# A Hyena mixer with a mixture of experts on one core: where the norm of half of the tokens and the filter steps stand

## Chip, core and metric

The kernel runs on one core of a Trainium2 chip. The metric is the device time of one execution in microseconds (us). The engines are TensorE (PE, with its weight loads listed as PEld), VectorE (DVE), ScalarE (ACT), GpSimd (POOL) and SyncE (SP), which issues most of the DMAs. Each engine works through its own queue in order.

## What is computed

One layer on 2048 tokens of width 1024: positional embedding, adaLN norm, a Hyena mixer (projection to three streams, a convolution of three taps, two long convolutions by FFT with filters that a small network generates), then a mixture of experts. The part that matters here, cut from the reference:

```python
x = x + _grid_pos_embed(rows, D_MODEL)[None]
m_l = jnp.split((jax.nn.silu(c) @ mod_w[i] + mod_b[i])[:, None, :], 6, -1)
hl = _layer_norm(x, ADALN_EPS) * (1.0 + m_l[1]) + m_l[0]
u = _centred_conv3(hl @ w_in + b_in, conv_w, conv_b)          # 1024 -> 3072
v, x1, x2 = jnp.split(u, 3, -1)
# filters: a = sin(...) three times, h = (a @ f_w3) * window, two-sided, divided by its L1 norm, rfft
z = x2 * long_conv(x1 * long_conv(v, 0), 1)
x = _ln_affine(DEEPNORM_ALPHA * x + (1.0 + m_l[2]) * (z @ w_out + b_out), ln_g, ln_b)
```

## The kernel before

Matmuls that need float32 accuracy are made of three matmuls on a high and a low part (`mm3`); `split_const` makes the parts: a cast on ACT, then a subtraction on DVE. Work that is to overlap is written as Python generators which a driving loop advances step by step, so the order of each engine's queue is the order in which the loops call `next`.

The front of the kernel has four pieces:

- `filter_acts` and `early_mod`: the filter's small network and the first two rows of the modulation, with 32 loads of its weights.
- `side_steps`: the norm of the tokens. `norm` takes two tiles of 128 tokens by 1024 at a time (a group; eight groups): it loads x and the column part of the positional embedding (`pc`) by SP, adds two embeddings on POOL, takes statistics on DVE (`ln_stats`, `rstd` with a Sqrt on ACT) and scales the tile on DVE. `turn` transposes a group on PE into PSUM, ACT applies the modulation (`ht`), and the tokens of the first half (quarters 0 and 1) are split into `hh` and `hl` in SBUF, while those of the second half go to DRAM (`h2d`) by SP.
- `filter_steps`: 64 product steps (`gen`: eight matmuls `g`, DVE's product with the window `gw`, absolute values on ACT `ab`, sums `acc` on DVE and POOL, sum and difference `hb` on POOL and DVE) and 64 transform steps (`tran`: four matmuls `sp`, ACT's copy `ev`, stores to `fud`); after eight of each, `norms` adds the sums up. Each `yield` is a step; there are some 139 by the kernel's own count.
- `phase_in`: the input projection. Its first half (stage A in this text) goes over 24 blocks of 128 output columns (`project`: per block 2 x 8 x 3 matmuls into `ip`); a block has four slots, each after 12 matmuls, in which `slot` advances other work: the filter's rest and then `open_B`, the split of the next block's weights (`split_w`) and `post`, which convolves, transposes and stores the block before. Then the second half does the same with the tokens that `open_B` fetched from `h2d`.

Before, `build` runs all of `side_steps` and 104 filter steps beside it, ahead of `phase_in`; the 35 that are left, and then the ten steps of `open_B`, go over stage A's first 90 slots. From `phase_in` on the order is the written one (`manual_schedule`); ahead of it the compiler may reorder. PSUM: `f_ps` has two buffers each of `g` and `sp`, `sd_ps` two for transposes, `i_psA` two each of `ip` and `tp`.

Of the kernel before, what the change touches and what calls it, by code (L numbers as in the profile page):

```python
# [12 lines left out]
F32 = mybir.dt.float32  # L13
F32R = mybir.dt.float32r
# [3 lines left out]
AF = mybir.ActivationFunctionType  # L18
OP = mybir.AluOpType
# [9 lines left out]
ADALN_EPS = 1e-6  # L29
# [3 lines left out]
ES = 2  # L33
MB = 8
MV = 2
XB = 7
ENDA = 90
NF0 = 104
VB = 2
L1 = 2  # L40
L2 = 1
# [127 lines left out]
def split_const(nc, hi, raw, lo):  # L169
    nc.scalar.copy(hi, raw)  # L170
    nc.vector.tensor_tensor(lo, raw, f_(hi), OP.subtract)  # L171
# [309 lines left out]
        yield  # L481


def side_steps(tc, A, md, sg, ident, S, ones_f, ps, h2d, mod):


    nc = tc.nc
    hA = S.st.enter_context(tc.tile_pool(reuse_waits="tile", name="hA", bufs=1, side="right"))
    xv = A["x"][0].rearrange("(n1 n2) d -> n2 n1 d", n2=16)

    def norm(wk, grp):
        stat = wk.tile([128, 2, 2], F32, name="stat")
        xs = []
        for j in range(2):
            n2 = grp * 2 + j
# [10 lines left out]
        r = wk.tile([128, 2], F32, name="r")  # L506
        nb = wk.tile([128, 2], F32, name="nb")
        rstd(nc, wk, r, nb, stat, ADALN_EPS, 2)
        for j in range(2):
            nc.vector.tensor_scalar(xs[j], xs[j], r[:, j:j + 1], nb[:, j:j + 1], op0=OP.mult, op1=OP.add)  # L510
            yield
        ready.append((grp, xs))

    def turn(wk):
        grp, xs = ready.pop(0)
        q, h = divmod(grp, 2)
        if grp in (0, 2):
            S.hh.append(S.x16.tile([128, 8, 512], F32R, name="x") if q == 0 else hA.tile([128, 8, 512], F32R, name="hh"))
            S.hl.append(S.x16.tile([128, 8, 512], F32R, name="x") if q == 0 else hA.tile([128, 8, 512], F32R, name="hl"))
        cols = slice(h * 256, h * 256 + 256)  # L520
        for t in range(0, 8, 2):
            p = ps.tile([128, 2, 256], F32, name="sd")
            ht = wk.tile([128, 2, 256], F32, name="ht", bufs=2)
            for i in range(2):
                for j in range(2):
                    nc.tensor.transpose(out=p[:, i, j * 128:j * 128 + 128], in_=xs[j][:, (t + i) * 128:(t + i) * 128 + 128],
                                        identity=ident)
                nc.scalar.activation(ht[:, i], p[:, i], AF.Identity, scale=md[:, 1, t + i:t + i + 1],
                                     bias=md[:, 0, t + i:t + i + 1])
            if q < 2:  # L530
                split_const(nc, S.hh[q][:, t:t + 2, cols], ht, S.hl[q][:, t:t + 2, cols])
            else:
                nc.sync.dma_start(h2d[q - 2, :, t:t + 2, cols], ht)
            yield

    ready = []
    with tc.tile_pool(reuse_waits="tile", name="h_wk", bufs=2, side="right") as wk:
# [4 lines left out]
        yield  # L542
        for _ in mod:
            next(first, 0)
        for _ in first:
            pass
        for grp in range(8):
            nx = norm(wk, grp + 3) if grp < 5 else iter(())
            for n, _ in enumerate(turn(wk)):
                next(nx, 0)  # L550
                next(nx, 0)
                yield
            for _ in nx:
                yield
    S.wpA = S.st.enter_context(tc.tile_pool(reuse_waits="tile", name="i_wA", bufs=2, side="right"))
    S.w = split_w(nc, S.wpA, load_w(nc, A, S.wpA, S.cts[0]))


def load_w(nc, A, wp, ct):
# [12 lines left out]
def phase_in(tc, A, S, filt, fst, fps, invn, sg, rowd, wod, ident, ones_f, h2d, ued, ud, x1d, x2d):  # L572

# [3 lines left out]
    nc = tc.nc  # L577
    with ExitStack() as st:
# [11 lines left out]
        r = wkA.tile([128, 2, 128], F32, name="cv", bufs=3)  # L590
# [119 lines left out]
        more = filt_then_B()  # L710
        late = None
        for n, ct in enumerate(cts):
            nxt = []

            def slot(i):
                nonlocal raw
                at = 4 * n + i
# [12 lines left out]
        while active:  # L730
            step()
        for _ in more:
            pass
        stA.close()
        S.st.close()

# [965 lines left out]
def build(tc, A, out):  # L1702
    nc = tc.nc
    with ExitStack() as st:
# [25 lines left out]
        with tc.tile_pool(reuse_waits="tile", name="i_cst", bufs=1) as S.top, ExitStack() as S.st, ExitStack() as fst:  # L1730
            fps = S.st.enter_context(tc.tile_pool(reuse_waits="tile", name="f_ps", bufs=2, space=PSUM))
            fcst = fst.enter_context(tc.tile_pool(reuse_waits="tile", name="f_cst", bufs=1))
            afw = fcst.tile([128, T], F32R, name="afw")
            arv = fcst.tile([128, T], F32R, name="arv")
            with tc.tile_pool(reuse_waits="tile", name="sd_ps", bufs=2, space=PSUM) as sps:
                pools = [fst.enter_context(tc.tile_pool(reuse_waits="tile", name="f_in", bufs=2))]
                filt = filter_steps(tc, A, fcst, pools, fps, afw, arv, invn, fud)
                with tc.tile_pool(reuse_waits="tile", name="f_ld", bufs=1) as ld, \
                        tc.tile_pool(reuse_waits="tile", name="m_wk", bufs=2) as mk:
# [4 lines left out]
                    side = side_steps(tc, A, md, sg, ident, S, ones_f, sps, h2d, mod)  # L1744
                    for n, _ in enumerate(acts):
                        next(mod, 0)
                        if n == 15:
                            next(filt)
                        if n == ES:
                            next(side)  # L1750
                    next(side)
                pools.append(fst.enter_context(tc.tile_pool(reuse_waits="tile", name="f_wk", bufs=2)))
                S.left = 139
                for n, _ in enumerate(side):
                    for _ in range((n + 1) * NF0 // 28 - n * NF0 // 28):
                        next(filt)
                        S.left -= 1
            phase_in(tc, A, S, filt, fst, fps, invn, sg, rowd, wod, ident, ones_f, h2d, ued, ud, x1d, x2d)
# [32 lines left out]
```

## Time and profile before

| | us |
|---|---|
| median of three runs | 4122.95 |
| lowest, highest | 4119.94, 4126.99 |
| the profiled execution | 4124.47 |
| its span, first to last instruction | 4122.70 |

The profile is one execution. The table of stretches gives each engine's busy time in a stretch, the granted clock of PE (1.00 is 2.4 GHz), the mean busy share of the 16 DMA engines and the rate. Groups by line show how often an operation ran, its busy time and the mean of one in ns. Waits tell which engine stood idle and whose instruction released it. The timeline shows single instructions; the recorded end of a matmul is modelled, so the distance between starts tells more than its length.

### The profile page before, as it was taken

The numbers are of one execution on the slowest core, as the hardware profiler recorded it, in microseconds if no ns is written. First come the engines' busy times: TensorE is split into PE (matmuls) and PEld (weight loads), VectorE is DVE, ScalarE is ACT, GpSimd is POOL, SyncE is SP. The second block draws the span as 40 slices with busy tenths as digits, with TensorE's granted clock in tenths as the row PEclk, the third lists the DMA queues.
The fourth block names the chain that finished last, engine by engine and source line by source line (L and its number), as shares of the span: only waits on it lengthen the run. The fifth ranks groups of instructions, "written<-read, shape, count | busy, mean of one in ns | idle before, by whom it ended". The sixth has DMA issues, their size and how long they took to land.

```text
span 4122.7 us, 53152 instructions
## 1 busy us (share of the span) xinstructions
PE 3857.8 (94%) x19830; PEld 3163.6 (77%) x19830; DVE 2798.6 (68%) x4044; ACT 1959.5 (48%) x2897; POOL 1077.3 (26%) x1106
## 2 busy tenths in 40 slices
PE   6788999999999998947999999999999999999997
PEld 2445787777777887736888888888888888888896
DVE  6997544776977776785666666666666666656666
ACT  4555332333777652123555555555555555544443
POOL 4674221222577542130000000000000000015635
PEclk7999999999999999978999999999999999999999
DMA  7666454666989996444656665666566666656764
GB/s 192 184 207 180 125 160 165 198 206 199 289 252 276 266 288 194 158 164 135 205 195 206 198 200 194 204 204 194 195 204 204 194 198 202 204 191 210 240 228 163
DMA packets 645822, 831.75 MB, mean 202 GB/s; under 512 B 56883, under 2 KB 532803, under 8 KB 643260
## 3 DMA queue, kind: packets, MB, share of 16 engines
q1 hardware_dynamic: 576066, 678.56, 51.8%
q0 software_dynamic: 52512, 146.97, 12.2%
q10 hardware_dynamic: 16986, 2.83, 0.4%
q8 instruction: 156, 2.56, 0.3%
q14 instruction: 102, 0.84, 0.1%
HBM read 643.82 MB, written 150.75 MB: 193 GB/s over the span
## 4 chain that ended last, share of the span: by engine, by line
PE 73%; DVE 10%; issue 5%; POOL 5%; DMA 4%; ACT 2%; SPq 0%; ACTq 0%; POOLq 0%; DVEq 0%
PE ab L1491 19%; PE ab L1492 10%; PE acc L175 5%; PE acc L176 5%; PE acc L177 5%; PE ip L175 4%; PE ip L177 4%; PE ip L176 4%; PE op L175 1%; PE op L177 1%; PE op L176 1%; PE sp L336 1%; PE ab L177 1%; PE ab L176 1%; PE ab L175 1%
## 5 line engine op out<-in xcount | busy, mean ns | idle before, releaser
L1491 PE MATMUL ab<-xs,w3h 128*128 128x512 f32 x1664 | 600.4, 399 | 0.0
L1491 PE MATMUL ab<-xs,w1h 128*128 128x512 f32 x1664 | 598.0, 399 | 0.0
L1390 DVE TENSOR_TENSOR w2l<-w2r,w2h 128x2048 fp32r<-128x2048 f32 x126 | 297.5, 2361 | 267.2 <-ACT w2h L1389 267.2
L1492 PE MATMUL ab<-xs,w3l 128*128 128x256 f32 x1664 | 468.2, 281 | 0.0
L1492 PE MATMUL ab<-xs,w1l 128*128 128x256 f32 x1664 | 466.5, 280 | 0.0
L175 PE MATMUL acc<-w2h,hh 128*128 128x512 f32 x1024 | 404.2, 395 | 14.5 <-ACT hh L170 13.8
L176 PE MATMUL acc<-w2l,hh 128*128 128x512 f32 x1024 | 402.5, 393 | 0.0
L177 PE MATMUL acc<-w2h,hl 128*128 128x512 f32 x1024 | 399.8, 391 | 0.8 <-DVE hl L171 0.8
L1491 PEld LDWEIGHTS ab<-xs,w3h 128*128 128x128 f32 x1664 | 313.0, 188 | 76.4
L1491 PEld LDWEIGHTS ab<-xs,w1h 128*128 128x128 f32 x1664 | 313.0, 188 | 72.8
L1537 POOL DMA_INDIRECT accd<-y,idx x27 | 68.4, 2533 | 1103.1 <-DVE y L1531 1096.8
L1390 DVE TENSOR_TENSOR w1l<-w1r,w1h 128x2048 fp32r<-128x2048 f32 x126 | 300.9, 2388 | 62.7 <-ACT w1h L1389 62.5
L170 ACT CAST hh<-u 128x256 fp32r<-128x256 f32 x256 | 104.1, 407 | 479.1 <-DVE u L1514 479.1
L1492 PEld LDWEIGHTS ab<-xs,w1l 128*128 128x128 f32 x1664 | 314.2, 189 | 7.1
L1492 PEld LDWEIGHTS ab<-xs,w3l 128*128 128x128 f32 x1664 | 314.8, 189 | 0.0
L1495 DVE TENSOR_TENSOR u<-ab,u 128x256 f32<-128x256 f32 x416 | 174.6, 420 | 204.2 <-ACT u L1494 195.9
L1390 DVE TENSOR_TENSOR w3l<-w3r,w3h 128x2048 fp32r<-128x2048 f32 x126 | 292.9, 2324 | 19.0 <-ACT w3h L1389 19.0
L1389 ACT CAST w2h<-w2r 128x2048 fp32r<-128x2048 f32 x128 | 244.1, 1907 | 96.1 <-PE acc L177 86.5
L1389 ACT CAST w1h<-w1r 128x2048 fp32r<-128x2048 f32 x128 | 244.5, 1910 | 80.2 <-PE ab L1491 79.0
L1389 ACT CAST w3h<-w3r 128x2048 fp32r<-128x2048 f32 x128 | 244.6, 1911 | 68.3 <-PE ab L1491 66.2
L175 PEld LDWEIGHTS acc<-w2h,hh 128*128 128x128 f32 x1024 | 193.1, 189 | 61.3 <-ACT hh L170 15.7
L1494 ACT COPY u<-ab 128x256 f32<-128x256 f32 x416 | 153.0, 368 | 183.0 <-PE ab L1492 182.9
(403 smaller groups left out, 9260.6 us busy)
## 6 DMA issues: line engine op xcount, KB each, us to landing
w1r<-in_moe_w_dram SPq DMA_DIRECT2D x128, 1024.0 KB
w3r<-in_moe_w_dram SPq DMA_DIRECT2D x128, 1024.0 KB
w2r<-in_moe_w_dram SPq DMA_DIRECT2D x128, 1024.0 KB
fud<-ev SPq DMA_DIRECT2D x128, 256.0 KB
kr<-fud SPq DMA_DIRECT2D x64, 512.0 KB
bn<-ao POOLq DMA_DIRECT2D x248, 128.0 KB, 7.1
mw<-in_mod_w_dram SPq DMA_DIRECT2D x96, 256.0 KB
wraw<-in_hy_w_in_dram SPq DMA_DIRECT2D x48, 512.0 KB
```

Of the source, the lines that this page charges most:

```text
L170: nc.scalar.copy(hi, raw)
L175: nc.tensor.matmul(out, lhsT=ah, rhs=bh, start=start, stop=False)
L176: nc.tensor.matmul(out, lhsT=ah, rhs=bl, start=False, stop=False)
L177: nc.tensor.matmul(out, lhsT=al, rhs=bh, start=False, stop=stop)
L336: nc.tensor.matmul(p, lhsT=s1[:, th], rhs=hb[th], start=True, stop=(n0 > 0))
L1389: nc.scalar.copy(h, raw)
L1390: eng.tensor_tensor(l, raw, f_(h), OP.subtract)
L1491: nc.tensor.matmul(p, lhsT=ws[2 * j][:, k, fs], rhs=xs[:, k], start=(k == 0), stop=False)
L1492: nc.tensor.matmul(p[:, 0], lhsT=ws[2 * j + 1][:, k, fs], rhs=xs[:, k, 0], start=False, stop=(k == 7))
L1494: nc.scalar.copy(u, p[:, 1])
L1495: nc.vector.tensor_tensor(u, p[:, 0], u, OP.add)
L1537: nc.gpsimd.indirect_dma_start(out=accd, out_offset=at(idx, h), in_=y, in_offset=None, compute_op=OP.add)
```

## The change

- Of `side_steps`, only quarters 0 and 1 (the first half of the tokens) come ahead of `phase_in`, with no filter step beside them. A quarter (four tiles) is normed at a time rather than two tiles; there are eight buffers for x rather than seven.
- The scaling of the norm moves from DVE (`tensor_scalar`) to ACT (`activation`, Identity with scale and bias).
- Quarters 2 and 3 become 29 steps in slots 0 to 21 of stage A; their transposes use `i_psA`'s `tp` buffers.
- All filter steps after the first (131 calls) go over slots 22 to 87; `open_B`'s ten over slots 88 to 95.
- The working tiles of the filter's network and the modulation move to the other side of SBUF, the first block's weights are loaded ahead and split during the turn of quarter 1, and the pool `hA` is opened by `build`.

The core of the diff (arguments that are only passed on are left out):

```diff
-XB = 7
-ENDA = 90
-NF0 = 104
+XB = 8
+SA = 22
+SF = 88
...
-    def norm(wk, grp):
-        stat = wk.tile([128, 2, 2], F32, name="stat")
+    def norm(quarter):
+        stat = wk.tile([128, 4, 2], F32, name="stat")
...
-            nc.vector.tensor_scalar(xs[j], xs[j], r[:, j:j + 1], nb[:, j:j + 1], op0=OP.mult, op1=OP.add)
-            yield
+            nc.scalar.activation(xs[j], xs[j], AF.Identity, scale=r[:, j:j + 1], bias=nb[:, j:j + 1])
+            yield 1
...
-        first = chain(norm(wk, 0), norm(wk, 1), norm(wk, 2))
-        next(first)
-        yield
-        for _ in mod:
-            next(first, 0)
-        for _ in first:
-            pass
-        for grp in range(8):
-            nx = norm(wk, grp + 3) if grp < 5 else iter(())
-            for n, _ in enumerate(turn(wk)):
-                next(nx, 0)
-                next(nx, 0)
-                yield
-            for _ in nx:
-                yield
+        for half in range(2):
+            first = norm(2 * half)
+            next(first)
+            yield 1
+            for _ in mod:
+                next(first, 0)
+            for _ in first:
+                if half:
+                    yield 1
+            nx = norm(2 * half + 1)
+            for n, _ in enumerate(turn(2 * half)):
+                next(nx, 0)
+                if n % 2:
+                    next(nx, 0)
+                yield 1
+            for _ in nx:
+                yield 1
+            for _ in turn(2 * half + 1):
+                yield 1
+            if half == 0:
+                yield None
...
+        psum[0] = lambda: psA.tile([128, 4, 128], F32, name="tp").rearrange("p (i j) c -> p i (j c)", i=2)
...
-        def filt_then_B():
-            yield from filt
+        def steps_of_A():
+
+            yield 0, SA, 29, side
+            open_filt()
+            yield SA, SF, 131, filt
             fst.close()
-            yield from open_B()
+            yield SF, 96, 10, open_B()
...
-                for _ in range((at + 1) * (S.left + 10) // ENDA - at * (S.left + 10) // ENDA):
+                a, b, count, more = part
+                for _ in range((at + 1 - a) * count // (b - a) - (at - a) * count // (b - a)):
                     next(more, 0)
+                if at == b - 1:
+                    for _ in more:
+                        pass
+                    part = next(plan, None)
...
+                S.wpA = S.st.enter_context(tc.tile_pool(reuse_waits="tile", name="i_wA", bufs=2, side="right"))
+                rawA = load_w(nc, A, S.wpA, S.cts[0])
+                for n, _ in enumerate(iter(lambda: next(side), None)):
+                    if n == 8:
+                        S.w = split_w(nc, S.wpA, rawA)
...
-                S.left = 139
-                for n, _ in enumerate(side):
-                    for _ in range((n + 1) * NF0 // 28 - n * NF0 // 28):
-                        next(filt)
-                        S.left -= 1
```

## Rows read from the trace of the kernel before

**Rows 1.** The page: span, and PE's busy tenths in 40 equal slices.

```profile
span 4122.7 us, 53152 instructions
...
PE   6788999999999998947999999999999999999997
```

**Rows 2.** Stretches: length, busy us (instructions) by engine, clock, DMA share, GB/s.

```profile
64.00:374.00 310.00, 236.83 (x932) 131.65 (x931) 290.19 (x388) 173.86 (x326) 213.72 (x137) 0.91 0.65 196
523.70:684.90 161.20, 161.20 (x749) 133.38 (x748) 77.12 (x115) 53.87 (x82) 34.29 (x50) 1.00 0.44 139
374.30:684.90 310.60, 309.46 (x1406) 248.25 (x1407) 149.84 (x213) 107.48 (x170) 76.98 (x97) 0.99 0.43 132
```

**Rows 3.** Stretches of the projection's own tile ip: PE, PEld and ACT busy.

```profile
523.70:684.90 161.20, 151.14 (x643) 118.90 (x642) 17.94 (x26) 1.00 0.44 139
```

**Rows 4.** PE's waits from 64 to 374 us: total us, times, longest.

```profile
PE g L295 <- DVE gw L298: 26.1, 25, 3.2
...
PE sp L336 <- POOL hb L312: 11.2, 15, 1.1
```

**Rows 5.** Timeline of PE at several moments: start us, us, instruction.

```profile
236.68 0.28 PE L296 MATMUL g<-wl,afw 128*128 128x256 f32 x1
236.80 0.28 PE L295 MATMUL g<-wh,afw 128*128 128x256 f32 x1
...
378.21 0.63 PE L175 MATMUL ip<-x,wh 128*128 128x512 f32 x1
378.63 0.63 PE L176 MATMUL ip<-x,wh 128*128 128x512 f32 x1
...
385.19 1.02 PE L336 MATMUL sp<-hb,s 128*128 128x512 f32 x2
...
498.66 1.89 PE L319 MATMUL g<-acc,onec 128*1 128x256 f32 x8
...
502.30 0.60 PE L614 MATMUL tp<-ident,cv 128*128 128x128 f32 x4
...
519.67 0.59 PE L336 MATMUL sp<-hb,s 128*128 128x512 f32 x1
```

**Rows 6.** Groups by line, 64 to 374 us: busy us, mean ns, idle before.

```profile
L312 DVE TENSOR_TENSOR hb<-gw,gw 128x512 f32<-128x512 f32 x58 | 78.7, 1357 | 0.2
L298 DVE TENSOR_TENSOR gw<-g,win 128x512 f32<-128x512 f32 x118 | 76.6, 673 | 6.6 <-PE g L296 6.4
...
L276 DVE TENSOR_TENSOR acc<-acc,ab 128x512 f32<-128x512 f32 x50 | 50.8, 1017 | 1.3 <-ACT ab L308 1.3
...
L528 ACT ACTIVATE ht<-sd,md 128x256 f32<-128x256 f32 x64 | 35.5, 565 | 31.5 <-PE sd L526 18.0 <-DVE hl L171 7.9 <-DVE x L171 4.9
...
L510 DVE TENSOR_SCALAR x<-x,r,nb 128x1024 f32<-128x1024 f32 x16 | 20.6, 1325 | 0.0
...
L170 ACT CAST x<-ht 128x512 fp32r<-128x512 f32 x8 | 4.8, 616 | 0.2
```

**Rows 7.** Line L312, whole span: ns shortest/median/longest, first and last start.

```profile
L312 DVE TENSOR_TENSOR hb<-gw,gw x64: 676/1750/1780, 65.5 to 473.7; 128x512 f32<-128x512 f32 x64
L312 POOL TENSOR_TENSOR hb<-gw,gw x64: 1260/1654/2262, 65.5 to 473.3; 128x512 f32<-128x512 f32 x64
```

**Rows 8.** Timeline near the first norm: POOL's adds, DVE's first scaling.

```profile
60.67 1.26 POOL L500 TENSOR_TENSOR x<-x,pr 128x512 f32<-128x512 f32 x1 [2.31 <-DMA x<-in_x_dram]
...
68.50 1.26 POOL L500 TENSOR_TENSOR x<-x,pr 128x512 f32<-128x512 f32 x1
...
70.94 1.26 POOL L500 TENSOR_TENSOR x<-x,pr 128x512 f32<-128x512 f32 x1
...
77.63 2.90 DVE L510 TENSOR_SCALAR x<-x,r,nb 128x1024 f32<-128x1024 f32 x2
```

**Rows 9.** Line L1569, the same scaling at the kernel's end: ns shortest/median/longest.

```profile
L1569 ACT ACTIVATE xs<-xs,nb,r x20: 1225/1236/1246, 3710.0 to 4069.5; 128x1024 f32<-128x1024 f32 x20
```

**Rows 10.** Tile hr, the second half's tokens fetched in stage A.

```profile
L695 SPq DMA_DIRECT2D hr<-h2d x8: 320/532/1001, 527.6 to 588.2; - x8
```

More of the change, by code (lines that the diff above doesn't have):

```diff
@@ L481, in early_mod, with side_steps @@
         yield
-def side_steps(tc, A, md, sg, ident, S, ones_f, ps, h2d, mod):
+def side_steps(tc, A, md, ident, S, psum, h2d, mod):
     nc = tc.nc
-    hA = S.st.enter_context(tc.tile_pool(reuse_waits="tile", name="hA", bufs=1, side="right"))
     xv = A["x"][0].rearrange("(n1 n2) d -> n2 n1 d", n2=16)
-    def norm(wk, grp):
-        stat = wk.tile([128, 2, 2], F32, name="stat")
+    def norm(quarter):
+        stat = wk.tile([128, 4, 2], F32, name="stat")
         xs = []
-        for j in range(2):
-            n2 = grp * 2 + j
+        for j in range(4):
+            n2 = quarter * 4 + j
             x = wk.tile([128, 1024], F32, name="x", bufs=XB)
@@ L512, in norm @@
[L512 to L533, printed above, removed]
-            yield
@@ new lines, in norm, with turn @@
+            yield 1
+        r = wk.tile([128, 4], F32, name="r")
+        nb = wk.tile([128, 4], F32, name="nb")
+        rstd(nc, wk, r, nb, stat, ADALN_EPS, 4)
+        for j in range(4):
+            nc.scalar.activation(xs[j], xs[j], AF.Identity, scale=r[:, j:j + 1], bias=nb[:, j:j + 1])
+            yield 1
+        ready.append(xs)
+    def turn(q):
+        xs = ready.pop(0)
+        if q < 2:
+            S.hh.append(S.x16.tile([128, 8, 512], F32R, name="x") if q == 0 else S.hA.tile([128, 8, 512], F32R, name="hh"))
+            S.hl.append(S.x16.tile([128, 8, 512], F32R, name="x") if q == 0 else S.hA.tile([128, 8, 512], F32R, name="hl"))
+        for h in range(2):
+            cols = slice(h * 256, h * 256 + 256)
+            for t in range(0, 8, 2):
+                p = psum[0]()
+                ht = wk.tile([128, 2, 256], F32, name="ht", bufs=2)
+                for i in range(2):
+                    for j in range(2):
+                        nc.tensor.transpose(out=p[:, i, j * 128:j * 128 + 128],
+                                            in_=xs[2 * h + j][:, (t + i) * 128:(t + i) * 128 + 128], identity=ident)
+                    nc.scalar.activation(ht[:, i], p[:, i], AF.Identity, scale=md[:, 1, t + i:t + i + 1],
+                                         bias=md[:, 0, t + i:t + i + 1])
+                if q < 2:
+                    split_const(nc, S.hh[q][:, t:t + 2, cols], ht, S.hl[q][:, t:t + 2, cols])
+                else:
+                    nc.sync.dma_start(h2d[q - 2, :, t:t + 2, cols], ht)
+                yield 1
@@ L536, in side_steps @@
     ready = []
-    with tc.tile_pool(reuse_waits="tile", name="h_wk", bufs=2, side="right") as wk:
+    with tc.tile_pool(reuse_waits="tile", name="h_wk", bufs=2) as wk:
         pr = wk.tile([128, 512], F32, name="pr", bufs=1)
         nc.sync.dma_start(pr, A["c_posr"])
-        first = chain(norm(wk, 0), norm(wk, 1), norm(wk, 2))
-        next(first)
-        yield
-        for _ in mod:
-            next(first, 0)
-        for _ in first:
-            pass
-        for grp in range(8):
-            nx = norm(wk, grp + 3) if grp < 5 else iter(())
-            for n, _ in enumerate(turn(wk)):
+        for half in range(2):
[9 more added lines that the diff above has]
+            for n, _ in enumerate(turn(2 * half)):
@@ L550, in side_steps @@
                 next(nx, 0)
-                next(nx, 0)
-                yield
+                if n % 2:
+                    next(nx, 0)
+                yield 1
             for _ in nx:
-                yield
-    S.wpA = S.st.enter_context(tc.tile_pool(reuse_waits="tile", name="i_wA", bufs=2, side="right"))
-    S.w = split_w(nc, S.wpA, load_w(nc, A, S.wpA, S.cts[0]))
+                yield 1
+            for _ in turn(2 * half + 1):
+                yield 1
+            if half == 0:
+                yield None
@@ L703, in open_B @@
                     yield
-        def filt_then_B():
-            yield from filt
+        def steps_of_A():
+            yield 0, SA, 29, side
+            open_filt()
+            yield SA, SF, 131, filt
             fst.close()
-            yield from open_B()
-        more = filt_then_B()
+            yield SF, 96, 10, open_B()
+        plan = steps_of_A()
+        part = next(plan)
         late = None
@@ L731, in phase_in @@
             step()
-        for _ in more:
-            pass
         stA.close()
@@ L1734, in build @@
             arv = fcst.tile([128, T], F32R, name="arv")
+            S.hA = S.st.enter_context(tc.tile_pool(reuse_waits="tile", name="hA", bufs=1, side="right"))
             with tc.tile_pool(reuse_waits="tile", name="sd_ps", bufs=2, space=PSUM) as sps:
@@ L1737, in build @@
                 filt = filter_steps(tc, A, fcst, pools, fps, afw, arv, invn, fud)
-                with tc.tile_pool(reuse_waits="tile", name="f_ld", bufs=1) as ld, \
-                        tc.tile_pool(reuse_waits="tile", name="m_wk", bufs=2) as mk:
+                psum = [lambda: sps.tile([128, 2, 256], F32, name="sd")]
+                with tc.tile_pool(reuse_waits="tile", name="f_ld", bufs=1, side="right") as ld, \
+                        tc.tile_pool(reuse_waits="tile", name="m_wk", bufs=2, side="right") as mk:
                     mod = early_mod(nc, A, md, sg, ident, ones_f, mk, sps)
```

12 lines of the change are left out of this document (5 added, 7 removed).

## The prediction

> **What bounds the kernel now.** The page comes first: TensorE (PE) is busy in nine tenths of the span except in a few slices, and the widest gap lies in slices 1 to 4, the first 400 us [rows 1]. Nothing in the diff touches code that runs after the input projection's first half, so I cut that front into stages by the table of stretches. Two stages matter. The *side stage*, 64 to 374 us, runs the norm of all 2048 tokens, its transposes and most of the filter: there VectorE (DVE) is busy 290.19 of 310 us and PE's records cover 236.83 [rows 2]. *Stage A*, 374.3 to 684.9 us, is the projection of the first half of the tokens with what is left of the filter: PE is busy 309.46 of 310.60 us, DVE only 149.84 [rows 2]. So DVE bounds the one, PE the other, and each leaves the other engine's time unused.
>
> A busy PE is not a full PE, so I price PE's work by the distance between starts. A projection matmul costs, its share of transposes and first DFT included, 161.20 us over 643 of them, 0.2507 us, in the stretch without filter [rows 2, 3]; 1152 cost 289 us. A filter matmul of 256 columns starts 0.12 us after the one before, two of 512 columns end 1.02 us after the start of the first, where one takes 0.59, so 0.43 apart; eight of the norm sums take 1.89, 0.22 each [rows 5]. The whole filter is 512 x 0.118 + 256 x 0.43 + 64 x 0.216 and some 14 us of one-row matmuls: 198 us. A transpose is about 0.11 [rows 5]. In the side stage lie 58 of 64 product steps (hb x58 [rows 6]), with 468 + 224 + 56 of those matmuls and 12 us, and 128 transposes: 189 us of work in 310. **PE has 121 us of slack there**, and its longest waits are for gw, which DVE makes, and for hb of POOL [rows 4]. That slack is what can be won.
>
> **The change, part by part.** *Lead-in.* Before the first projection matmul only quarters 0 and 1 of the tokens (8 tiles of 1024 columns) are still normalised and turned; no filter step stands among them. GpSimd (POOL) starts on the second tile at 60.67 and needs 1.26 for each of two adds, 2.44 a tile at its best [rows 8]: the eighth is done near 78, the fourth near 68. Its statistics and the reciprocal root of the quarter follow; before, the first scaling began at 77.63, for want of the slow small DVE operations beside POOL's adds [rows 8]. I take 75. From there ScalarE (ACT) is last. The scaling that it takes over from DVE costs 1.24 by the same operation at the kernel's end [rows 9], against 1.33 on DVE [rows 6]; 8 tiles are 9.9 us. A turn step is two scalings of 0.57 and a cast of 0.62 [rows 6]; 16 steps are 28 us. With the cast of the first weights, 39 us: 114, and 3 us for gaps between steps, so the projection starts at **117** rather than 374.3. Bounds: 110 if the root is ready at 71 and nothing gaps, 125 if each step waits 0.4 us more for PE and DVE. The loads of these tiles (6 MB) are no later than before, in the same order on SyncE's queue.
>
> *Stage A.* It now carries the projection (289), the whole filter (198) and 64 transposes (7): **494 us of PE work**, 183 more than the 311 now. If PE never waited, it would end at 117 + 494 = 611 against 684.9. What it waits for, in the order of the slots (a slot is 12 projection matmuls, 3.0 us):
>
> - The clock. Before, after the thinly filled side stage, projection matmuls stood 0.42 apart instead of 0.23 for a few us [rows 5]; eight of them cost 1.6 us. After a thinner lead-in the same: 2.
> - Slots 0 to 21 hold the second half's 29 side steps: 16 x loads and positional loads on SyncE behind the weight loads, POOL's adds ahead of POOL's DMA issues for the projection, statistics on DVE ahead of the weight split and the convolution, and 16 stores of turned tiles on SyncE. DVE stands in order behind POOL behind a DMA. Slots last 3.2 us and DVE's own share is near 2.2 (149.84 over 96 slots is 1.6, and 8 tiles' statistics at some 1.6 us over 22 slots are 0.6), so a late tile delays it by some us, once or twice. The bounds are 0 and 12; I take 5.
> - Slots 22 to 87 hold all filter steps, one product step and one transform step a slot. PE needs 66 x 3.0 + 198 = 396 us. DVE: a product step is two gw at 0.67, one hb and seven eighths of an acc at 0.68 undisturbed [rows 6, 7], with small things 2.8 us, 181 for 64; the projection's own DVE work is stage A's 149.84 less its filter and hB splits (34), two thirds of it 80. On top comes what POOL takes from DVE: hb is 0.68 alone and 1.75 beside a POOL operation [rows 7], 1.36 and 1.02 on the mean for hb and acc [rows 6], so 58 x 0.68 + 50 x 0.34 = 56 us lost over 108 POOL operations, 0.52 each. There are 120 in the new stretch: 62 at that rate, 128 if each blocks DVE in full (1.07). Small operations and the scaling lost time as well, so I take 85. DVE is 346 of 396, 87%, at most 389. In the side stage DVE reached 94%, so PE should keep the lead; for slots in which weight split, convolution and product step meet I add 14 us (bounds 3 and 40). ACT (174 + 107 busy in the two stages [rows 2], plus 20 for scaling) has half of the time free. DMA traffic is 310 x 196 + 311 x 132 GB/s, 102 MB, now in 575 us: 177 GB/s, under the 196 of the side stage.
> - Slots 88 to 95 hold the 10 steps that fetch and split the second half's turned tokens. Before, the fetches were issued from 527.6 to 588.2 [rows 10]; now in 24 us, with two buffers, by 8 casts on ACT's queue ahead of the projection's evacuations. Bounds 0 and 16; I take 7.
>
> That is 28 us: stage A ends at 117 + 494 + 28 = 639, **46 us earlier**. After it nothing changes. The scaling's removal from DVE (16 x 1.33 = 21 us) is worth nothing by itself in stage A and is in the lead-in already.
>
> A page speaks against the overlap: the Trainium skill, "SBUF — State Buffer", section "SBUF: two separate sides", says that the port pair shared by VectorE and GpSimd is an exclusive lock, so that the second to come blocks until the first is through. The rows agree with the lock (0.68 against 1.75). By the rule, a POOL add could hold DVE for the whole of its 1.26 us, and the two-input convolution operations would be exposed as well; 120 such blocks would be 151 us, DVE 412, and at 94% a stretch of 438 in place of 410: 4106 instead of 4078. The DVE-bound rival below is this mechanism, priced from rows alone.
>
> **The rivals.** *Clean overlap.* PE never waits beyond the lower bounds: start at 113, 10 us of waits, end 617, gain 68: 4057. For it: in stage A before, PE lost 2 us in all although filter steps ran beside it (309.46 of 310.60 [rows 2]). Against it: there were a quarter as many per slot.
>
> *DVE becomes the bound of the filter's slots.* POOL blocks it in full, DVE has 389, and at the side stage's 94% the slots last 416; PE's own waits (20) do not fall together with DVE's. With the start at 122 and 14 elsewhere: 122 + 494 + 40 + 14 = 670, gain 15: 4110.
>
> *PE stalls in every slot (slower).* The mechanism is order: in each slot PE's queue holds transform and product matmuls that need hb, gw's buffers and ev of the slots before, and while it waits, the projection matmuls behind cannot pass. In the side stage this cost 121 us for 58 product steps, 2.1 each. If each of 64 slots lost 2.1 us, 134 us in place of 14, the end would be 759: 4199. It decides from 54 us more than I count, 0.8 us a slot more. Against it: a product step's results are wanted a slot (6 us) later here, where in the side stage they were wanted at once, with DVE behind.
>
> *The change does not shorten the front*, because the loads of x and not the norm set the start: then 6 MB at the side stage's 196 GB/s, 31 us from 56, end at 87, ahead of ACT's 114. So this decides nothing.
>
> **How the numbers follow.** The profiled execution took 4124.47, 1.8 us outside its span, 1.5 over the median of the three runs (4122.95). 4124.5 - 46 = 4078.5; I say 4078. Chances: forecast 0.52, clean overlap 0.20, DVE-bound 0.20, stalls in every slot 0.08. Range: from 4055 (just past the clean case) to 4112 (past the DVE-bound one); what is left out is the slower case, and little on either side. Faster or slower counts from 0.2%, 8 us, about what a measurement of this kernel can tell from no change. Forecast and clean overlap are faster; of the DVE-bound case three quarters are. Faster 0.87, within 0.2% 0.05, slower 0.08.
>
> **What would show it.** Right: projection matmuls (ip) from 110 to 125 on; PE busy throughout from there to about 640; the filter's first hb near 190 and its last fud store near 610; DVE at 85 to 92% in between; PE's waits for gw, hb and ev under 15 us in total. A start later than 125 would put the error in the lead-in; waits of PE for DVE in most slots would speak for the DVE bound; a hole of 10 us or more near 640, before the second half's first matmul, for the fetches crowded into slots 88 to 95. I would be wrong altogether if stage A took more than 568 us.

## The result and the profile after

The changed kernel takes 4152.94 us (4150.83 to 4157.21) against 4123.88 of the kernel before in the same comparison: ratio 1.0072, interval 1.0055 to 1.0090. It is **29 us slower**, where the prediction said 46 faster. The profiled execution of after took 4150.83, with a span of 4148.5.

The page of after, its span, PE's busy tenths and PE's granted clock in 40 slices of 104 us, answers to [rows 1]:

```profile
span 4148.5 us, 53057 instructions
...
PE   5689998999999998966999999999999999999997
...
PEclk7899999999999998987999999999999999999999
```

The gap of slices 1 to 4 has become shorter and deeper (5, 6, 8 instead of 6, 7, 8, 8), and a dip at the seventh slice (8, from 622 to 726 us) is new; the notch at the eighteenth is in both. So the front was shortened, and yet the end came later: the loss lies in that slice and where the digits read 9, too fine for this view. The table of stretches, cut at the prediction's stages, shows it (columns as in [rows 2]):

```profile
64.00:115.40 51.40, 19.60 (x65) 9.35 (x65) 31.44 (x58) 35.34 (x59) 20.82 (x16) 0.50 0.43 143
115.40:240.00 124.60, 91.21 (x401) 71.58 (x402) 40.27 (x76) 47.88 (x79) 29.62 (x31) 0.89 0.38 120
240.00:680.00 440.00, 413.08 (x1809) 287.30 (x1808) 330.79 (x402) 207.00 (x358) 225.44 (x181) 0.97 0.55 166
680.00:703.00 23.00, 18.59 (x75) 15.01 (x74) 10.98 (x14) 7.99 (x10) 2.60 (x4) 0.85 0.58 184
703.00:760.00 57.00, 45.04 (x194) 35.33 (x193) 33.00 (x56) 16.51 (x24) 7.33 (x11) 0.91 0.77 265
```

The projection starts at 115.4 (predicted 117). Then PE stands still for 33 us in slots 0 to 21, for 26 in the filter's slots, for 4.4 in slots 88 to 95 (a transpose that waits for DVE's `cv`, at 691.6) and for 10 at the start of the second half. DVE, which could have been the bound of the filter's slots, is busy 330.79 of 440 us there, 75%: neither engine is full. The milestones, as predicted and in the trace of after, in us:

| | predicted | after | difference |
|---|---|---|---|
| first projection matmul | 117 | 115.4 | -2 |
| slots 0 to 21 | 80 | 119.8 (to 235.2) | +40 |
| slots 22 to 87 | 410 | 443.5 (to 678.7) | +33 |
| slots 88 to 95, up to the second half's first matmul | 31 | 29.6 (to 708.3) | -1 |
| from there to the second half's second block | 13.1, as before | 21.5 (to 729.8) | +8 |

The waits of PE in after, by stretch (115.4 to 240, 240 to 680, 680 to 760 us; total us, times, longest), stand beside those of [rows 4]:

```profile
PE tp L525 <- ACT ht L527: 26.3, 16, 9.6
PE sp L175 <- ACT vh L626: 6.6, 1, 6.6
...
PE g L319 <- DVE acc L276: 26.3, 8, 6.0
PE g L295 <- DVE gw L298: 0.3, 1, 0.3
...
PE ip L175 <- ACT ub L672: 10.5, 1, 10.5
```

These are three kinds of place, and gw, which led [rows 4] with 26.1 us, is down to 0.3. At each of them a short dependent step stands in PE's in-order queue, with projection matmuls ready behind it; whether the engines lack time all the same is what the experiments ask.

**Slots 0 to 21.** Each step of the turn issues two transposes, ACT's scaling of them, two more transposes into the other half of the same PSUM tile, and ACT's scaling again. The timeline of after at one step, with nothing else late (start us, us, engine, line, operation; in brackets the idle time before it and what ended it):

```profile
163.88 0.54 PE L525 MATMUL tp<-ident,x 128*128 128x128 f32 x2
...
164.46 0.56 ACT L527 ACTIVATE ht<-tp,md 128x256 f32<-128x256 f32 x1 [4.01 <-PE tp L525]
...
165.08 0.44 PE L525 MATMUL tp<-ident,x 128*128 128x128 f32 x2 [0.66 <-ACT ht L527]
```

The second pair can't start until ACT has read the first: about 1 us from start to start, 16 times, once for each step of the second half's turn. The Trainium skill, "PSUM — Partial Sum Buffer", section "PSUM bank collisions raise a hardware error", says why such a wait can't just be dropped: one engine may not write a PSUM bank while another reads it in the same partitions, whichever columns they touch (the tile is 4 x 128 float32 a partition, 2 KiB, by that page one bank). The trace agrees: ACT's read ends at 165.02, the next transpose starts at 165.08.

When ACT is late as well, the step costs far more. The longest such wait is 9.6 us, from 185.8 on. The other long wait of the stretch has the same chain, here from its beginning:

```profile
135.24 0.38 SPq L564 DMA_DIRECT2D wraw<-in_hy_w_in_dram  x1
...
135.71 0.53 SPq L496 DMA_DIRECT2D x<-in_x_dram  x1
...
140.37 1.26 POOL L499 TENSOR_TENSOR x<-x,pr 128x512 f32<-128x512 f32 x1 [7.25 <-DMA x<-in_x_dram]
...
141.67 0.69 DVE L378 BATCH_NORM_STATS2 bst<-x 128x6 f32<-128x512 f32 x1 [3.06 <-POOL x L499]
...
145.55 1.24 ACT L509 ACTIVATE x<-x,nb,r 128x1024 f32<-128x1024 f32 x1 [1.28 <-DVE nb L397]
146.70 0.56 ACT L626 CAST vh<-tp 128x512 fp32r<-128x512 f32 x1
...
147.31 0.80 PE L175 MATMUL sp<-vh,s1h 128*128 128x512 f32 x1 [6.60 <-ACT vh L626]
```

x is issued behind a weight load, POOL adds when it lands, DVE takes statistics, ACT waits in order for their root and then does the moved scaling, and only then the cast that PE wants. The cast has nothing to do with the norm; it is merely behind it on ACT.

**Slots 22 to 87.** All eight waits for acc are the norm sums, one for each of the filter's blocks. The timeline of after around one of them:

```profile
387.56 1.21 DVE L171 TENSOR_TENSOR wl<-wraw,wh 128x1024 fp32r<-128x1024 f32 x1
...
390.06 0.75 DVE L642 SCALAR_TENSOR_TENSOR cv<-ub,prm,cv 128x512 f32<-128x512 f32 x1
390.72 1.28 DVE L298 TENSOR_TENSOR gw<-g,win 128x512 f32<-128x512 f32 x2
...
391.71 1.28 POOL L276 TENSOR_TENSOR acc<-acc,ab 128x512 f32<-128x512 f32 x1
391.92 2.83 DVE L276 TENSOR_TENSOR acc<-acc,ab 128x512 f32<-128x512 f32 x1
...
392.93 1.26 POOL L312 TENSOR_TENSOR hb<-gw,gw 128x512 f32<-128x512 f32 x1
...
394.90 3.57 PE L319 MATMUL g<-acc,onec 128*1 128x256 f32 x8 [6.05 <-DVE acc L276]
```

DVE has the split of the projection's weights and the convolution ahead of the block's last gw and sum, and PE's next instruction is the sum over that sum. A filter block is eight product and eight transform steps, at two steps a slot eight slots, which is two projection blocks of four slots: so **every** block's last sum meets the same two jobs. The eight waits differ all the same, from 0.6 to 6.0 us.

**The boundary.** The fetches of the second half's tokens and the weights behind them on SP's queue, in after:

```profile
680.59 29.88 SPq L699 DMA_DIRECT2D hr<-h2d  x8
...
710.52 1.05 SPq L753 DMA_DIRECT2D x<-in_c_s_dram  x1
...
712.15 0.67 SPq L564 DMA_DIRECT2D wraw<-in_hy_w_in_dram  x1
...
728.16 1.04 ACT L170 CAST wh<-wraw 128x1024 fp32r<-128x1024 f32 x1 [11.94 <-DMA wraw<-in_hy_w_in_dram]
```

The same weights and cast in before:

```profile
686.24 0.43 SPq L561 DMA_DIRECT2D wraw<-in_hy_w_in_dram  x1
...
702.28 1.04 ACT L170 CAST wh<-wraw 128x1024 fp32r<-128x1024 f32 x1 [10.56 <-DMA wraw<-in_hy_w_in_dram]
```

Before, the last fetch was issued at 588.2 [rows 10] and the weights for the second half's second block 4.6 us ahead of that half's first matmul; now the fetches go on to 710.5 and the weights follow at 712.15, 3.8 us behind that matmul (708.3). ACT waits for them with an evacuation of ip behind, and PE waits 10.5 for that evacuation instead of 2.1. The late issue is one half of this. The other is that these weights need 16 us from issue to cast in both traces, where the page of after gives a median of 4.1 from issue to landing for this load over the whole kernel: right ahead of them on SP's queue go two tables of 2 MB each (`in_c_s`, `in_c_a`), in before too. That they wait for those tables is likely and was not tested.

### The profile page after: what moved, and what is told of

It reads as the page before. It is cut to its first block, busy times and chain, and to the rows that moved or that the text cites. A ratio compares the mean times of both kernels' runs of the same rounds, so it can differ in the third digit from the quotient of the medians.

```text
span 4148.5 us, 53057 instructions
## 1 busy us (share of the span) xinstructions
PE 3856.6 (93%) x19830; PEld 3169.5 (76%) x19830; DVE 2780.3 (67%) x4000; ACT 1980.2 (48%) x2909; POOL 1066.3 (26%) x1106
## 3 DMA queue, kind: packets, MB, share of 16 engines
q10 hardware_dynamic: 16986, 2.83, 0.5%
## 4 chain that ended last, share of the span: by engine, by line
PE 70%; DVE 11%; issue 6%; POOL 5%; DMA 5%; ACT 3%; SPq 0%; POOLq 0%; ACTq 0%; DVEq 0%
PE ab L1503 19%; PE ab L1504 9%; PE acc L175 5%; PE acc L176 5%; PE acc L177 5%; PE ip L175 3%; PE ip L177 3%; PE ip L176 3%; PE sp L336 2%; PE op L175 1%; PE op L177 1%; PE op L176 1%; PE ab L177 1%; PE ab L176 1%; PE ab L175 1%
## 5 line engine op out<-in xcount | busy, mean ns | idle before, releaser
L175 PE MATMUL ip<-hh,wh 128*128 128x512 f32 x576 | 235.8, 409 | 10.5 <-ACT ub L672 10.5
```

Source lines behind the costliest of these rows:

```text
L175: nc.tensor.matmul(out, lhsT=ah, rhs=bh, start=start, stop=False)
```

## The experiments

Two theories. **Order**: the work fits, and PE stands at the few places above, because a short dependent step is next in its queue. Then a change of order alone, with the same work, brings the time back. **Load**: there is too much for DVE, POOL and ACT beside PE in stage A, and order moves the waits about but not the sum. A difference below is taken against the 4152.94 of after, and a ratio with its interval against the kernel before of the same round. The intervals reach 4 to 7 us to either side, so a difference of a few us is not told from none.

### Both pairs of transposes ahead of ACT's scalings

```diff
                         nc.tensor.transpose(out=p[:, i, j * 128:j * 128 + 128],
...
+                for i in range(2):
                     nc.scalar.activation(ht[:, i], p[:, i], AF.Identity, scale=md[:, 1, t + i:t + i + 1],
```

> The kernel after, with one edit: in a turn step all four transposes are issued before ACT's two scalings, not two and two. Theory Order (PE stands in its queue behind short dependent steps): of 26.3 us of PE's waits for ht in slots 0 to 21, about 17 are the second pair of a step waiting for ACT's read of the first pair in the same PSUM tile; they go, with some 5 us of half clock behind them, and the lead-in loses up to 5: 20 to 27 us faster than the kernel after, 4126 to 4133. Theory Load (the engines beside PE cannot keep up with what was moved, and PE waits wherever it stands): the same wait turns up at the next transposes or casts, gain under 5, at least 4148.

4140.36 us, ratio 1.0034 (1.0022 to 1.0045): **13 us** back, between the two. The sixteen waits are gone from PE's list, and the filter's first matmul comes at 223.4 instead of 238.1. Some of it moved: the late x now shows in waits for the low part vl (6.1 us at 168.9) and for cv (6.8 at 190.7), which had cost next to nothing in these slots, beside the 6.8 for vh, so Order's size was about twice what came.

### x of the later quarters loaded ahead

```diff
+    def load(n2):
+        x = wk.tile([128, 1024], F32, name="x", bufs=XB)
+        nc.sync.dma_start(x, xv[n2])
+        return x
...
+    def norm(quarter, ahead=False):
...
+        if ahead:
+            got = [load(quarter * 4 + j) for j in range(4)]
...
+            yield 1
...
+            for n, _ in enumerate(turn(2 * half + 1)):
+                if half == 0 and n == 3:
+                    ahead = norm(2, True)
+                    next(ahead)
```

Quarter 2's x goes out in the turn of quarter 1, quarter 3's in slot 0; the positional loads run two tiles ahead.

> The kernel after, with one edit: the loads of x of quarters 2 and 3 are issued ahead (quarter 2's during the turn of quarter 1, quarter 3's in slot 0), the positional columns two tiles ahead, so that they do not stand behind the projection's weight loads on SyncE. Theory Order: the two long waits in slots 0 to 21 (7.0 us at 140, 9.9 at 186) are a late tile that holds POOL, DVE, ACT and then PE; they go, with 5 us of half clock: 15 to 22 faster, 4131 to 4138. Theory Load: DVE and ACT are late by their own work; gain under 5, at least 4148.

4140.67, ratio 1.0035 (1.0023 to 1.0046): **12 us** back, somewhat under the expected 15 to 22. PE's wait for vh falls from 6.6 to 1.2, the longest within a turn step from 9.6 to 3.1; fifteen short ones remain, and the norm sums are as they were (27.3 us). The filter starts at 228.7.

### The filter's steps two slots earlier

```diff
-SA = 22
-SF = 88
+SA = 20
+SF = 86
```

Not one instruction is added or taken away; only the slot in which each filter step meets the projection's.

> The kernel after, with all filter steps two slots earlier (slots 20 to 85 instead of 22 to 87); nothing else. The last sums of a filter block are then issued in slot 3 of a projection block, where DVE has neither the weight split nor the convolution of four rows, rather than in slot 1 behind both. Theory Order (the norm matmuls wait because DVE's sum stands behind that block's other work): PE's 26 us of waits at the eight norms fall under 10, with 8 us of half clock behind them, and the boundary gets 6 us more: 25 to 35 faster, 4118 to 4128. Theory Load (DVE and POOL are slow throughout the filter's slots): waits as long, only at other slots, and the crowded side steps (29 in 20 slots) cost some: 4148 to 4158. The variant with later norm matmuls was slower since their PSUM tile is one of gw's two, so PE then stood behind gw of the same slot; this one leaves that order alone.

4120.26, ratio 0.9992 (0.9982 to 1.0001): **33 us** back, the number that Order said, and level with the kernel before. Its waits of PE from 64 to 760 us, two lines:

```profile
PE tp L525 <- ACT ht L527: 18.7, 16, 5.0
...
PE g L319 <- DVE acc L276: 10.5, 5, 2.6
```

The 66 slots of the filter in after, then in this run (columns as in [rows 2]):

```profile
235.20:678.70 443.50, 416.58 (x1827) 290.32 (x1827) 334.47 (x408) 208.05 (x359) 226.30 (x182) 0.97 0.56 167
```

```profile
223.20:656.30 433.10, 412.92 (x1823) 289.90 (x1821) 337.31 (x407) 208.59 (x360) 227.50 (x182) 0.99 0.56 170
```

The waits for the norm sums cost 10.5 instead of 26.3, with as many slots and as much work as in after. But only a part of the gain lies there. In the profiled execution (4126.28, 24.5 less than that of after) the filter's slots give 10.4 of it, since new waits for gw, invn and ev (8.5 together) take some back. The rest lies in the side steps, whose waits for ht fell too (18.7 instead of 26.3), in the last slots and at the boundary (7.2 instead of 10.5). So the size came out as Order said, partly at other places than it named. That order alone, with the same instructions, brings 33 us back speaks against Load most plainly.

### The three together

```diff
-SA = 22
-SF = 88
+SA = 20
+SF = 86
...
+                for i in range(2):
...
+                    ahead = norm(2, True)
```

> The kernel after with three edits together: transposes of a turn step issued in one go, x of quarters 2 and 3 loaded ahead, filter steps two slots earlier. Theory Order: the three waits are separate places in PE's queue, so the gains add: 13 and 12 as measured and 25 to 35 for the phase, 48 to 60 faster than the kernel after: 4093 to 4105, faster than the kernel before. Theory Load: one lack shows up at three places, the gains do not add: at least 4125.

4096.4, ratio 0.9931 (0.9914 to 0.9947): 56.5 us less than after, where 13, 12 and 33 add to 58. **The three gains add**, as far as the intervals tell. The stretches of slots 0 to 19 (up to the filter's first matmul) and of the filter:

```profile
111.60:199.40 87.80, 77.30 (x364) 62.24 (x365) 37.47 (x67) 44.33 (x77) 27.61 (x29) 0.96 0.46 145
199.40:626.00 426.60, 409.48 (x1812) 287.94 (x1812) 335.91 (x409) 207.48 (x357) 226.91 (x180) 0.99 0.57 173
```

and two of PE's waits from 64 to 760 us:

```profile
PE g L319 <- DVE acc L276: 8.8, 5, 2.6
PE ip L175 <- ACT ub L697: 8.4, 1, 8.4
```

DVE does about the same work in less time (335.91 of 426.60 us, 79% against 75%), and PE waits less. Load would have it the other way. The mean granted clock in these two stretches is 0.96 and 0.99 where after has 0.89 and 0.97.

### The norm sums issued a step later

```diff
-        yield
         m = n - GA
-        if 0 <= m + 1 < 64 and steps[m + 1][1] == 7:
-            sums_of = norms(steps[m + 1][0])
+        if m >= 0 and steps[m][1] == 7:
+            sums_of = norms(steps[m][0])
             next(sums_of)
+        yield
         if m >= 0:
             tran(m)
```

> The kernel after, with one edit: the eight matmuls that add up a block's absolute sums (norms) are issued one step later, behind the product step and not ahead of the transform step, so DVE and POOL have some 3 us more (and the next product step's time) for the last sums. Theory Order: PE's 26.3 us of waits for acc go nearly all, and about 10 us of half clock that follows them: 28 to 36 faster, 4117 to 4125. Theory Load (DVE is the bound of the filter's slots): PE waits as long at other places, for gw or hb; gain under 8, at least 4145.

4163.55, ratio 1.0086 (1.0069 to 1.0103): **11 us slower** than after by the medians (6 by the ratios, whose intervals overlap), and no gain in any case; the expectation missed. PE's waits from 64 to 760 us say why:

```profile
PE g L319 <- DVE gw L298: 31.4, 7, 6.0
...
PE g L295 <- DVE gw L298: 4.9, 7, 1.6
```

The sums now come behind the next step's eight product matmuls, and their PSUM tile is one of the two named g. They no longer wait for acc but for DVE to empty a g that has just been filled. A wait moved along the same queue met the next dependence; that the sums wait for the block's last acc is only the first of two.

### All four quarters ahead, the filter over slots 0 to 87

```diff
-            if half == 0:
-                yield None
+    yield None
...
-            yield 0, SA, 29, side
             open_filt()
-            yield SA, SF, 131, filt
+            yield 0, SF, 131, filt
```

> The kernel after with all four quarters normalised and turned ahead of the projection (no side steps in stage A) and the filter's 131 steps over slots 0 to 87, 1.5 a slot. It separates the two things that the change moved into stage A. The lead-in grows by 8 scalings and 32 half steps on ACT, 28 us, plus gaps: start near 147. Theory Order: the 51 us of excess in slots 0 to 21 go, the norm waits fall since a block's sums have more time at 1.5 steps a slot: 25 to 45 faster than the kernel after, 4108 to 4128. If the filter's slots are what is slow at any density (Load): their excess of 44 us stays, gain 10 to 20, 4133 to 4143.

4143.54, ratio 1.0046 (1.0029 to 1.0062): 9 us better than after, and Order's number missed; it lies at the edge of Load's. The trace tells which term failed: the projection starts at 164.3, 49 us later than in after for two more quarters. PE's waits from 64 to 760 us:

```profile
PE sd L525 <- ACT ht L527: 43.6, 35, 5.5
...
PE g L319 <- DVE acc L276: 19.4, 7, 4.3
```

In a lead-in with nothing beside it, the turn's PE and ACT steps take turns and their waits are path. And the norm sums still wait 19.4 us, though the filter runs at 1.5 steps a slot instead of 2: thinning the load by a quarter doesn't remove them, which two slots of shift brought to 10.5. So the run speaks for neither theory by its time, and for Order by its waits.

### The scaling's engine

Three kernels. After, with the scaling back on DVE:

```diff
-            nc.scalar.activation(xs[j], xs[j], AF.Identity, scale=r[:, j:j + 1], bias=nb[:, j:j + 1])
+            nc.vector.tensor_scalar(xs[j], xs[j], r[:, j:j + 1], nb[:, j:j + 1], op0=OP.mult, op1=OP.add)
```

> The kernel after, with the norm's scaling put back on DVE. If ACT's queue is what holds the lead-in (ACT-bound by my sum) and the transposes of slots 0 to 21 (ht behind four scalings of 1.24 us), the start comes up to 8 us earlier and the wait of 9.6 us at 186 shrinks by 3: 6 to 12 us faster than the kernel after, 4141 to 4147. If DVE beside POOL's adds is as slow at it (1.33 us each before), nothing: within 4 of 4153.

4140.86, ratio 1.0040 (1.0026 to 1.0054): **12 us** less than after. The projection starts 1.4 us sooner (114.0), and the filter 9.6 sooner (228.5): the gain is for the most part in slots 0 to 21, where ACT has ht and the projection's evacuations behind the scaling and DVE has little to do.

The kernel before, with that one edit the other way round (DVE to ACT, two tiles at a time):

```diff
-            nc.vector.tensor_scalar(xs[j], xs[j], r[:, j:j + 1], nb[:, j:j + 1], op0=OP.mult, op1=OP.add)
+            nc.scalar.activation(xs[j], xs[j], AF.Identity, scale=r[:, j:j + 1], bias=nb[:, j:j + 1])
```

> The kernel before, with one part of the change alone: the norm's scaling on ACT rather than DVE. Theory DVE-bound side stage: 16 scalings of 1.33 us leave DVE's 290 of 310 us; 14 to 21 faster, 4103 to 4110. Rival (the chain through PE, POOL and ACT is as long as DVE's work, or ACT's queue order delays ht and ev): within 5 of the kernel before.

4118.3, ratio 0.9981 (0.9972 to 0.9991): **7.6 us faster** than before. The projection starts at 368.5 instead of 374.3. That lies between the two expectations: of some 21 us of work taken from DVE a third came back, so DVE was not the only bound of the side stage, or ACT's added work took the rest. The same edit is a gain there, and a loss where DVE has time.

The three reorderings with the scaling on DVE:

```diff
-            nc.scalar.activation(xs[j], xs[j], AF.Identity, scale=r[:, j:j + 1], bias=nb[:, j:j + 1])
+            nc.vector.tensor_scalar(xs[j], xs[j], r[:, j:j + 1], nb[:, j:j + 1], op0=OP.mult, op1=OP.add)
```

> The three edits together (transposes in one go, x ahead, filter two slots earlier: 4096) and the norm's scaling on DVE. On the kernel after, the scaling on DVE alone gave 12 us, by ACT's queue in slots 0 to 21. If that is a place of its own, it adds: 4082 to 4090. If it acted only through the waits for ht that the one-go transposes have removed, nothing is left: 4092 to 4100.

**4090.85**, ratio 0.9922 (0.9905 to 0.9938): 5.5 below the three alone, between the two expectations, 33 us under the kernel before and 62 under after. With most of the waits behind ACT already gone, the second engine is worth at most half of its 12: the intervals of the two versions overlap. This is the best version found.

### The filter earlier still, the fetches over fourteen slots

```diff
-SA = 20
-SF = 86
+SA = 16
+SF = 82
```

> The three edits together, with the filter in slots 16 to 81 (the same place within a projection block) and open_B's ten steps over slots 82 to 95, 14 slots instead of 10. Theory on the boundary: PE's 8.4 us before the second half's second block are weights queued behind eight fetches that SyncE still issues when the second half begins; with 12 us more they are out, and 5 to 8 us go: 4088 to 4092. Against it: 29 side steps in 16 slots make those waits longer by as much, no gain: 4094 to 4100. If the fetches do not matter and the 4 MB of tables loaded there do, the 8 us stay.

4099.36, ratio 0.9941 (0.9925 to 0.9958): 3 us more than the three together, which is within the noise: no gain. It was to free SP's queue before the boundary, but the ten steps are spread up to the last slot wherever they begin. The timeline at its boundary:

```profile
659.47 1.33 SPq L589 DMA_DIRECT2D wraw<-in_hy_w_in_dram  x1
...
676.75 1.04 ACT L170 CAST wh<-wraw 128x1024 fp32r<-128x1024 f32 x1 [12.37 <-DMA wraw<-in_hy_w_in_dram]
...
678.44 0.79 PE L175 MATMUL ip<-hh,wh 128*128 128x512 f32 x1 [7.56 <-ACT ub L697]
```

The weights go out 0.4 us ahead of the second half's first matmul (659.8), and PE waits 7.6. Over three traces the wait follows that lead: 4.6 ahead gives 2.1 (before), 0.4 ahead 7.6, 3.8 behind 10.5 (after). What hardly changes is the time from issue to cast, 16.0, 17.3 and 16.0, with the two tables just ahead each time. That is a pattern and no proof; neither a version whose fetches end early nor one with the tables elsewhere was tried.

## Why the prediction was wrong

**Right.** The lead-in: 115.4 against 117. Its chain was ACT's scaling and turn, as worked out, but the closeness is partly luck: the first scaling came at 77.7 and not at 75, and the rest took 38 us rather than 42. Nor was ACT alone the limit, since without the scaling it started the projection only 1.4 sooner. After the boundary nothing changed (the second half's last matmul comes 319.1 us after its second block's first in after, 319.0 before). gw was not a wait. DVE was not the bound of the filter's slots: 334 us of work where the prediction had 346, so POOL's blocking was, if anything, counted too high. The rival of a DVE bound was wrong in mechanism. The rival of a stall in every slot had the right kind of mechanism, a queue in order whose ready projection matmuls cannot pass, and the wrong place: PE stalled in one of the filter's slots in eight, for a sum that no rival named.

**The step that failed is the 28 us for what PE waits for.** The prediction compared averages, DVE's 346 us of work with PE's 396, ACT half free, and took from them how much a queue would wait. A wait in an in-order queue isn't set by the engines' averages but by what stands ahead of one instruction at one moment. Term by term:

- *Slots 0 to 21, 5 taken (bounds 0 to 12), 40 over.* The 119.8 us hold 73 of work, so 47 of something else: 33 are the waits listed above, and 13 are left for PE's lower clock (granted 0.89, after 0.50, the level of 1.2 GHz, in the stretch before) and lesser gaps. Seven had been counted for all this, two of them for the clock. The prediction saw the late x ("once or twice, some us") and not what was queued behind it on ACT. It overlooked the wait inside a turn step, though the trace of before had it. Its waits from 64 to 374 us:

```profile
PEld sd L526 <- ACT ht L528: 23.2, 24, 1.9
...
PE sd L526 <- ACT ht L528: 11.9, 16, 1.5
```

  In the side stage, with DVE busy 290.19 of 310 us [rows 2], these could hide, though no run shows how far they did. Moved into a stage where PE sets the end, they are path. The prediction counted the turn's transposes (7 us) and not the turn's dependence.
- *Slots 22 to 87, 14 taken (bounds 3 to 40), 33 over.* Of 47 us beyond the 396 of work, 26 are the eight norm sums. The prediction put 14 us on "slots in which weight split, convolution and product step meet" and so named the meeting, but not that every block's sum falls on it, nor that PE waits for the whole chain. Another 8 are the sums themselves. The groups of the norm sums from 190 to 690 us, of after and then of the three reorderings together (busy us, mean ns, idle before):

```profile
L319 PE MATMUL g<-acc,onec 128*1 128x256 f32 x64 | 23.1, 526 | 26.3 <-DVE acc L276 26.3
```

```profile
L319 PE MATMUL g<-acc,onec 128*1 128x256 f32 x64 | 15.1, 378 | 8.8 <-DVE acc L276 8.8
```

  After a wait of 4 to 6 us the sums run slowly: eight took 3.57 us after the wait at 388 against 1.89 in [rows 5], together 8 us (23.1 less 15.1). So a wait costs more than its length. The 13 that are left are probably work that was priced too low: the three reorderings, with 16 us of waits in their filter stretch of 426.6, have about as much over 396.
- *The boundary, 7 taken, 6 used and then 8 more.* The fetches did fit into slots 88 to 95. What they held up was the next thing on SP's queue, two tables and the second half's weights, and that fell beyond the end of the stage as the prediction drew it.
- *The scaling on ACT, taken at nothing in stage A.* It costs 12 us, most of it there: work moved to an engine with half of its time free is still ahead of what that engine's queue has next.
- *The end of stage A in before* was read at 684.9; its last matmul starts at 690.6, half a block later. With that end the prediction's own sum would have given a gain of 52. That slip hid 6 us of the error and caused none of it.

Together, -2 + 40 + 33 - 1 + 8 - 6 = 72 us, the difference between the 4078.5 of the sum and the profiled 4150.83. The prediction had named its limit: stage A over 568 us. It took 593.

The Trainium skill's lock of the port that VectorE and GpSimd share, "SBUF — State Buffer", "SBUF: two separate sides", was weighed in the prediction as a price of 120 blocked operations on DVE. The trace agrees with the lock, but DVE's total did not set the time; where a blocked sum reached PE was at two of the eight norm sums, the longest waits (6.0 us at 394.9, behind the 2.83 us in the chain above, and 5.4 at 558.1).

**What stays open.** The boundary's wait (8.4 us in the three reorderings, 7.2 in the best version) was explained in part and not removed. Nor was a PSUM tile of its own for the norm sums tried, which would tell whether issuing them later is worth something once they don't share g. Order is shown for the three edits that gave 56.5 us back, as a total; how much each place gave of the 33 us of the shift is known from one profiled execution alone. For the 8 us of the boundary it is argued.

## What to carry to other kernels

Before moving work under an engine that is the bound, list every wait of that engine on the moved work that is hidden now, and price each as path: here sixteen waits of about 1 us each cost 13 us once they stood in a stage that PE sets. Where two loops are interleaved and their periods divide each other, find the slot in which the tight dependence falls, and try a shift of a slot or two: here the same instructions two slots earlier were worth 33 us, some at the sums and some elsewhere. And look at what is next on the queue behind the moved work (SP's weights behind fetches, ACT's evacuations behind a scaling), since that is where the price is paid.

## What the hardware showed that was not expected

One DVE addition of 128x512 beside two POOL operations in a row took 2.83 us (391.92 to 394.75), against 0.68 undisturbed for an operation of that size [rows 7]: it waited through the second POOL operation too, which began 1.0 us after it. By the rule of the Trainium skill in the section named above it would have waited for the first one alone, to 392.99, and by an estimate from the 0.68 been through near 393.7; the measurement decides. It is not the only one. Of 25 of DVE's hb and acc operations in after that began under one POOL operation and saw a second begin, 19 were through 0.55 to 0.64 us after the first; six, all of them sums into acc, came out only behind the second, five of these with 2.83 to 2.85 us. In the run with all four quarters ahead one sum lay under three POOL operations, and was through 0.6 us after the last:

```profile
567.84 4.83 DVE L276 TENSOR_TENSOR acc<-acc,ab 128x512 f32<-128x512 f32 x1
```

What decides between the two outcomes no run here shows.

PE's mean granted clock was lower where PE waited more: 0.89 in the stretch with 33 us of waits, 0.96 in about the same slots of the three reorderings, where most of them were gone; 0.97 and 0.99 in the filter's slots.
